# A two-layer hybrid block on one core: attention woven into its own input projection, state matrices made in pieces, four-pass products made three rounded ones, one more weight buffer

## The chip, the cores and the metric

The kernel runs on one core of one Trainium2 chip. The metric is the device time of one execution in microseconds (us), from several runs of the same program. TensorE (PE in the profile) multiplies, VectorE (DVE) and ScalarE (ACT) do the element-wise work, GpSimd (POOL) clears buffers and issues a few transfers, SyncE (SP) issues the weight transfers.

## The reference, cut to what matters

Two layers work on 528 tokens (16 meta tokens and 512 inputs) of width 1024, all in 32-bit floats. Each layer is a mixer of three parallel parts, and an MLP with a squared ReLU:

```python
for l in range(2):
    a = rms_norm(h, norm_pre_mix[l])
    u, q, k, v, cq, ckv, kr = split(a @ w_in[l])          # 1024 -> 1376 columns
    y_ssm = s5_mixer(u, valid, ...)                       # linear recurrence, 16 groups x 64 states
    y_swa = swa_attention(q, k, v, sinks)                 # 8 heads, window 128, ALiBi, sinks
    y_mla = mla_mixer(cq, ckv, kr, pos, ...)              # 4 heads, low-rank q and kv, rope, causal
    mixed = concat(rms_norm(y_ssm), rms_norm(y_swa), rms_norm(y_mla))
    h = h + rms_norm(mixed @ w_out[l])                    # 1024 -> 1024
    a = rms_norm(h, norm_pre_mlp[l])
    h = h + rms_norm(square(relu(a @ w_mlp_up[l])) @ w_mlp_down[l])   # 1024 -> 4096 -> 1024
```

## The kernel before, in words

Tokens lie along the free axis, in two halves: A (272 tokens) and B (256). A weight matrix is cut into blocks of 128 output columns; a block is 8 tiles of 128x128, fetched by two transfers of 256 KB (`raw`). Per layer and half there are 11 blocks of input projection (`w_in`), 8 of output projection (`w_out`), and four MLP chunks of 8 blocks up and 8 down.

`gemm` (L137 to L163) computes one block in one of two ways. Where its input is plain 32-bit (`exact`), TensorE multiplies 8 pairs of tiles straight from `raw` (L153), in four passes each; the trace counts two records for one such product. Otherwise weight and input are each held as a rounded high part and a rounded rest, and TensorE does three products for each pair, 24 for a block (L161). `load_half` then has to split each half block of weights: ACT writes the rounded high part (L124, `w<-raw`), DVE the rest (L133). An input made for rounded products costs one or two more element-wise operations as well (`split`, L165 to L171).

The exact way is chosen by the tables at the top: FULL_IN (input projection of A and B in layer 0; of A the first NF = 9 blocks), FULL_OUT (output projection of A in both layers), FULL_C0 (first MLP chunk of A in both layers). That makes 33 exact blocks of 272 columns (9 + 8 + 8 + 3 + 5) and 35 of 256 (11 + 8 + 8 + 5 + 3).

`s5_prep` makes the state matrices and tables of the recurrence from the parameters alone, mostly with small DVE operations and a few PE transposes and products. It is called as one piece after the input projection of A (in `main`'s loop). `s5_half` (recurrence of one half) and `attn_half` (both attentions of one half) are generators: `weave` advances them beside a main stream of blocks, each by a rate (RS, RA) per block of the main stream. `weave(s1())` runs the input projection of B in layer 0 (WB = 11 blocks), or the second to fourth MLP chunk of B of layer 0 (`late`, 48 blocks, of which 6 run earlier) in layer 1, with the sides of half A; `weave(s2())` runs A's output projection, its residual and norms (`chain_mid`), the input projection of B in layer 1, and A's first MLP chunk, with the sides of half B. Sides begin only when the gate's stage is reached.

The order in each engine's queue is made by the framework's scheduler from the order in which the code issues, with a higher priority for the weight splits (HW) and for the norm chains (HP). Each engine then works through its queue in that order.

Of the kernel before, what the change touches and what calls it, by code (L numbers as in the profile page):

```python
# [20 lines left out]
P = 128  # L21
# [46 lines left out]
def hybrid(ctx, tc, xT, wblk, small, wglu, wuq, wukv, bD, cD, ident_d, bias_d, tbias_d, mask_d, rope_d, tau_d, outT):  # L68
# [7 lines left out]
    wsp = ctx.enter_context(tc.tile_pool(name="wsp", bufs=3))  # L76
# [102 lines left out]
    def tmp_p():  # L179
        return mk(wk, [P, 2, 272], F32, "wP", bufs=3)  # L180
# [59 lines left out]

    def s5_prep(L):
        l = L["l"]
# [4 lines left out]
        exp_acc(step, a, (s1, s2))  # L247
        V.tensor_tensor(a, sm(l, "are"), step, op=ALU.mult)
        exp_acc(r, a, (s1, s2))
        V.tensor_tensor(a, sm(l, "aim"), step, op=ALU.mult)  # L250
# [6 lines left out]
        V.tensor_tensor(plo, a, phi, op=ALU.subtract)  # L257
        tab = mk(mem, [P, 2, 8, TAB], F32, "tab")
# [7 lines left out]
        for i0 in range(0, 8, 4):  # L266
# [8 lines left out]
            V.scalar_tensor_tensor(x, km, MAGIC, x, op0=ALU.subtract, op1=ALU.subtract)  # L275
        act(tab[:, 0], tab[:, 1], AF.Sin, scale=TWO_PI / 2)
# [26 lines left out]
        V.tensor_tensor(ci, ci, den, op=ALU.mult)  # L303

# [18 lines left out]
        rs = mk(mem, [P, 8 * 68], F32, "rs")  # L323
        braw = flat(tmp_p(), 512).rearrange("p (c i j) -> p c i j", c=2, i=8)
# [3 lines left out]
        nci = chain_tmp()[0][:, :256].rearrange("p (i j) -> p i j", i=8)  # L328
        V.tensor_scalar(nci, vt[:, CL - 1, 1], -1.0, None, op0=ALU.mult)
        t3 = mk(psm, [P, 512], F32, "y")  # L330
        for i0 in range(0, 8, 4):
# [11 lines left out]
            for j in range(4):  # L343
                i = i0 + j
                for c, rhs in enumerate((vt[:, CL - 1, 0, i, :], nci[:, i, :])):
                    PE.matmul(t3[:, 32 * i:32 * i + 32], lhsT=ws[c][:, j].rearrange("p a b -> p (a b)"), rhs=rhs,
                              start=c == 0, stop=c == 1)
        t3v = t3[:, :256].rearrange("p (i j) -> p i j", i=8)
        act(tt[:, :, 3, :], t3v)
        for so in range(3):  # L350
            for q in range(so + 1):
                f = 32 * (q + 3 - so)
                act(tt[32 * q:32 * q + 32, :, so, :], t3v[f:f + 32])
        for m in range(CL):
# [3 lines left out]
        L["s5"] = dict(r4=r4, rs=rs, tab=tab, wt=wt, vt=vt, tt=tt)  # L358
# [26 lines left out]
    def new_layer(l):  # L385
        L = dict(l=l)
# [10 lines left out]
        return L  # L397

    def w_in(L, hf, ar, M):
# [5 lines left out]
        M["hf"] = hf  # L405
# [11 lines left out]
        for b in range(NB_IN):  # L417
            if l + hf == 0 and b == NF:
# [35 lines left out]
            yield  # L454
# [22 lines left out]
    def s5_half(L, M):  # L477
        l, hf = L["l"], M["hf"]
# [3 lines left out]
        tab, rs, r4 = s5["tab"], s5["rs"], s5["r4"]  # L482
        rv = rs[:, :8 * K].rearrange("p (i k) -> p i k", i=8)
        V.tensor_copy(rv, r4.unsqueeze(2).to_broadcast([P, 8, K]))
        V.memset(rv[:, :, 0:1], 0.0)
# [17 lines left out]
        for o in range(2):  # L503
# [13 lines left out]
            if hf == 1:  # L517
                it = mk(tiny, [P, 2, 4], F32, "init", bufs=1)
                for c in range(2):
                    V.tensor_tensor(it[:, c], sv[:, c, iq], r4[:, iq], op=ALU.mult)  # L520
                    w0 = iv(w_)[:, c, :, 0]
                    V.tensor_tensor(w0, w0, it[:, c], op=ALU.subtract if c else ALU.add)
            yield 2.7
            for c in range(2):
                V.tensor_tensor_scan(v_[:, c, :n], rs[:, 4 * o * K:4 * o * K + n], w_[:, c, :n], 0.0, op0=ALU.mult, op1=ALU.add)
# [75 lines left out]
    def attn_half(L, M):  # L601
        l, hf = L["l"], M["hf"]
# [21 lines left out]
        yield 0.5  # L624
        wq = []
# [23 lines left out]
        yield 1.0  # L649
        vt = mk(psm, [P, 512], F32, "s")  # L650
# [9 lines left out]
        units = [("swa", j, o, g) for j, o, _ in full for g in range(4)] + ([("swah", 0, 0, 0)] if head else [])  # L660
# [132 lines left out]
    def w_out(l, hf, mixed, o, b0, b1):  # L793
        n = span(l, hf)[1]
        for b in range(b0, b1):
            ps, = gemm(l, NB_IN + b, [(mixed, n)])
            act(o[:, b, :n], ps[:, :n])
            yield
# [28 lines left out]
    def up(l, c, st, b0=0, b1=8):  # L827
# [3 lines left out]
        for b in range(b0, b1):  # L831
# [10 lines left out]
            yield  # L842

    def down(l, c, st, b0=0, b1=8):
        for b in range(b0, b1):
# [7 lines left out]
            yield  # L853
# [22 lines left out]
    def weave(main, sides):  # L876
        due = [0.0 for _ in sides]
        for ready in main:
            for i, (g, rate, gate) in enumerate(sides):
                if ready < gate:  # L880
                    continue
                due[i] += rate
                while due[i] > 0:
                    c = next(g, None)
                    due[i] = -1e9 if c is None else due[i] - c
# [206 lines left out]
```

## Time and profile before

| what | value |
|---|---|
| median of 3 runs | 1330.17 us (1327.77 to 1330.74) |
| profiled execution | 1329.14 us, span 1327.3 us |
| PE busy | 1255.9 us, 95% of the span |
| DVE busy | 811.8 us, 61% |
| ACT busy | 793.1 us, 60% |
| mean granted PE clock | 0.978 of full speed |

The profiled execution is 1.0 us under the median. The span runs from the first to the last instruction; 1.8 us lie around it. PE, DVE and ACT work side by side, so their busy times do not add up; a stretch of the program takes at least as long as its busiest engine.

### The profile page before, as it was taken

Reading aid. Unit: us, or ns where it says so; the run is one execution under the profiler, and the core shown is the slowest. Engines: PE = TensorE matmul, PEld = TensorE weight load, DVE = VectorE, ACT = ScalarE, POOL = GpSimd, SP = SyncE. Lnnn points to the kernel's source line nnn. Section 1 sums busy time; section 2 is a strip of 40 time slices with the busy share of each in tenths; the row PEclk is TensorE's granted clock in tenths of the full one; section 3 lists DMA queues with packets and bytes.
Section 4 is the critical chain, followed back from the end, with each engine's and each line's share of the span. In section 5 each row is a group of like instructions: output and inputs, shape, how many; then the busy total and the mean of one; then the engine's idle time right before and its main releaser. Section 6 shows DMA issues by size and latency. Waiting matters only on the chain.

```text
span 1327.3 us, 26248 instructions
## 1 busy us (share of the span) xinstructions
PE 1255.9 (95%) x9784; PEld 1135.4 (86%) x9784; DVE 811.8 (61%) x2134; ACT 793.1 (60%) x1876; POOL 32.2 (2%) x66
## 2 busy tenths in 40 slices
PE   6899999799999999899999997999999999999995
PEld 5767775679999999898899987867789999999985
DVE  7766456475756566869777667454475333334776
ACT  5347647675866656756687656387666542534663
POOL 4001000010000000000000000000000000000000
PEclk9989999899999999899999998999999999999998
DMA  7322231235666666463344644312446433334663
GB/s 227 119 61 69 88 88 57 64 111 170 181 182 176 176 172 177 130 178 107 108 142 131 174 144 142 105 59 77 132 131 184 118 89 95 96 91 122 186 183 95
DMA packets 93231, 170.47 MB, mean 128 GB/s; under 512 B 10960, under 2 KB 14032, under 8 KB 93104
## 3 DMA queue, kind: packets, MB, share of 16 engines
q1 hardware_dynamic: 90288, 161.62, 42.0%
q0 software_dynamic: 2816, 7.18, 1.7%
q8 instruction: 77, 1.26, 0.4%
q14 instruction: 50, 0.41, 0.1%
HBM read 166.66 MB, written 2.10 MB: 127 GB/s over the span
## 4 chain that ended last, share of the span: by engine, by line
PE 83%; DVE 10%; ACT 5%; issue 1%; DMA 0%; DVEq 0%; ACTq 0%; POOLq 0%
PE d L161 47%; PE d L153 14%; PE bu L161 7%; PE o L754 3%; PE s L674 2%; PE pt L730 2%; ACT ch L124 2%; DVE big L781 2%; DVE h L782 2%; PE s L706 1%; ACT slot L124 1%; PE s L640 1%; DVE ch L198 1%; PE bu L508 1%; PE o L203 1%
## 5 line engine op out<-in xcount | busy, mean ns | idle before, releaser
L161 PE MATMUL d<-slot,w 128*128 128x256 f32 (+1 forms) x5568 | 702.4, 286 | 20.7 <-DVE slot L422 6.7
L161 PEld LDWEIGHTS d<-slot,w 128*128 128x128 f32 x5568 | 682.9, 191 | 31.6 <-ACT ch L124 6.9
L124 ACT ACTIVATE w<-raw 128x512 fp32r<-128x512 f32 x464 | 291.9, 629 | 271.6 <-PE d L161 192.0
L133 DVE TENSOR_TENSOR w<-raw,w 128x512 fp32r<-128x512 f32 x464 | 320.7, 692 | 211.1 <-ACT w L124 204.8
L153 PE MATMUL d<-slot,raw 128*128 128x256 f32 (+1 forms) x1088 | 273.3, 396 | 11.3 <-ACT ch L124 10.2
L153 PEld LDWEIGHTS d<-slot,raw 128*128 128x128 f32 x1088 | 205.3, 194 | 52.3 <-ACT ch L124 10.2
L161 PE MATMUL bu<-slot,w 128*128 128x256 f32 x768 | 93.5, 282 | 0.0
L161 PEld LDWEIGHTS bu<-slot,w 128*128 128x128 f32 x768 | 92.0, 190 | 0.0
L168 DVE TENSOR_TENSOR slot<-rl,slot 128x256 fp32r<-128x256 f32 (+1 forms) x112 | 47.3, 428 | 66.5 <-ACT slot L124 65.7
L198 DVE TENSOR_TENSOR ch<-ch 128x256 f32<-128x256 f32 (+1 forms) x112 | 48.1, 430 | 28.3 <-ACT ch L124 26.4
L124 ACT ACTIVATE rl<-d 128x256 f32<-128x256 f32 (+1 forms) x112 | 42.1, 376 | 34.4 <-PE d L153 17.6
L124 ACT ACTIVATE slot<-rl 128x256 fp32r<-128x256 f32 (+3 forms) x128 | 52.9, 421 | 2.8
L124 ACT ACTIVATE slot<-h,small 128x256 fp32r<-128x256 f32 (+3 forms) x88 | 39.8, 506 | 15.9 <-DVE h L782 12.2
L124 ACT ACTIVATE ph<-pt 128x512 f32<-128x512 f32 (+2 forms) x66 | 36.7, 556 | 20.4 <-PE pt L730 12.2
L124 ACT ACTIVATE rl<-rl 128x256 f32<-128x256 f32 (+1 forms) x112 | 46.1, 420 | 2.1
L852 DVE TENSOR_TENSOR big<-d,big 128x256 f32<-128x256 f32 (+1 forms) x80 | 34.3, 429 | 15.9 <-PE d L161 12.1
L674 PE MATMUL s<-kv,slot 128*128 128x512 f32 (+1 forms) x64 | 32.0, 582 | 0.8 <-ACT vs L124 0.7
L124 ACT ACTIVATE big<-d 128x256 f32<-128x256 f32 (+1 forms) x64 | 24.0, 375 | 13.7 <-PE d L153 7.3
L124 ACT ACTIVATE ch<-big 128x256 f32<-128x256 f32 (+1 forms) x64 | 26.4, 415 | 9.6 <-DVE big L852 7.4
L124 ACT ACTIVATE ch<-h 128x256 f32<-128x256 f32 (+1 forms) x64 | 24.9, 415 | 8.2 <-DVE ch L198 4.5
L782 DVE SCALAR_TENSOR_TENSOR h<-big,small,h 128x256 f32<-128x256 f32 (+1 forms) x64 | 28.5, 486 | 0.0
L706 PE MATMUL s<-kv,slot 96*128 96x264 f32 (+3 forms) x80 | 26.5, 413 | 0.3 <-DVE mx L585 0.3
(603 smaller groups left out, 1135.7 us busy)
## 6 DMA issues: line engine op xcount, KB each, us to landing
raw<-in_wblk SPq DMA_DIRECT2D x600, 256.0 KB, 2.7
ph<-in_wuq POOLq DMA_DIRECT2D x8, 256.0 KB, 3.0
h<-in_xT SPq DMA_DIRECT2D x4, 272.0 KB, 3.9
h<-in_xT SPq DMA_DIRECT2D x1, 1024.0 KB, 11.6
ph<-in_wukv POOLq DMA_DIRECT2D x4, 256.0 KB, 3.0
u<-in_wglu POOLq DMA_DIRECT2D x4, 256.0 KB, 3.0
out<-h SPq DMA_DIRECT2D x1, 1024.0 KB, 5.6
out<-h SPq DMA_DIRECT2D x4, 256.0 KB, 2.2
```

The source lines that it names most:

```text
L124: S.activation(out, in_, func, **kw)
L133: V.tensor_tensor(w[:, 1].rearrange("p k m -> p (k m)"), raw, f32(hi), op=ALU.subtract)
L153: PE.matmul(ps[:, :n], lhsT=raw[:, k * P:(k + 1) * P], rhs=a[:, 4 * q + k, :n], start=q + k == 0, stop=q + k == 4)
L161: PE.matmul(ps[:, :n], lhsT=w[:, wi, k, :], rhs=a[:, ai, 4 * q + k, :n], start=i == 0, stop=i == 23)
L168: V.tensor_tensor(lo, src, f32(hi), op=ALU.subtract)
L198: V.tensor_tensor(acc, acc, sq, op=ALU.add)
L674: PE.matmul(sp[:, :2 * nk].rearrange("p (e k) -> p e k", e=2), lhsT=M["q"][:, c0:c0 + P], rhs=L["k2"][:, :, ks:ks + nk], start=True, stop= ...
L706: PE.matmul(sp, lhsT=M["qh"][0:96, 2 * g + e, o:o + P], rhs=L["kh"][:, 2 * g + e, c0:c1], start=True, stop=True)
L730: PE.transpose(pt[:, 256 * x + P * e:256 * x + P * e + P], vs[e][:, c0:c0 + P], ident)
L754: PE.matmul(ops[64 * e:64 * e + 64, :P], lhsT=v, rhs=pp[:, P * e:P * e + P], start=i == 0, stop=i == len(ph) - 1, tile_position=(0, 64 * e))
L782: V.scalar_tensor_tensor(h[hf][:, k, o:o + n], src[:, k, :n], sm(l, gn, k), h[hf][:, k, o:o + n], op0=ALU.mult, op1=ALU.add)
L852: V.tensor_tensor(ac[:, b, :n], ps[:, :n], ac[:, b, :n], op=ALU.add)
```

## The change

- FULL_IN keeps only A of layer 0 (its first 9 blocks); FULL_OUT and FULL_C0 are empty. So 24 blocks of 272 columns and 35 of 256 go from eight four-pass products to 24 rounded ones, and their weights are split.
- The split weights have four buffers in place of three (`wsp`); one scratch buffer of the recurrence is given up for it (`tmp_p`), its factor row `rs` is made per half of the groups, and `s5_prep` uses parts of `vt` as scratch.
- `s5_prep` is a generator. In layer 0 it is a side of the first weave, ahead of `s5_half`; in layer 1 it is a side of the MLP stream that ends layer 0 (rate RP).
- The input projection of A is now the head of the first weave's main stream, and `attn_half` begins inside it: `wait` holds a side until the blocks that it needs are issued. ORD sets the order of blocks: for A the latent and key blocks first, the recurrence's (0, 1) last; for B the value block (10) ahead of the queries. Attention units go group by group.
- In layer 0 one block of B's input projection is left for after A's output projection (WB = 10). Side steps are paid by estimated time of the main stream (`cost`), with new rates.

```diff
-FULL_IN = ((0, 0), (0, 1))
-FULL_OUT = ((0, 0), (1, 0))
-FULL_C0 = ((0, 0), (1, 0))
-RS = ((2.4, 1.5), (0.75, 2.2))
-RA = ((2.76, 2.5), (0.92, 3.5))
+FULL_IN = ((0, 0),)
+FULL_OUT = ()
+FULL_C0 = ()
+RS = ((1.6, 0.5), (0.8, 0.8))
+RP = 0.25
+RA = ((0.8, 1.6), (0.35, 1.2))
+ORD = ((2, 3, 4, 5, 10, 6, 7, 8, 9, 0, 1), (0, 1, 2, 3, 4, 5, 10, 6, 7, 8, 9))
-WB = (11, 0)
+WB = (10, 0)
...
-    wsp = ctx.enter_context(tc.tile_pool(name="wsp", bufs=3))
+    wsp = ctx.enter_context(tc.tile_pool(name="wsp", bufs=4))
...
     def s5_prep(L):
+        yield 0.0
...
         exp_acc(step, a, (s1, s2))
+        yield 3.0
...
-        braw = flat(tmp_p(), 512).rearrange("p (c i j) -> p c i j", c=2, i=8)
+        braw = vt[:, 1]
...
-        for b in range(NB_IN):
-            if l + hf == 0 and b == NF:
+        for bi, b in enumerate(ORD[hf]):
+            if l + hf == 0 and bi == NF:
                 a, _ = gains(l, hf, 0, n, "g_in", False)
             ps, = gemm(l, b, [(a, n)])
...
-            yield
+            M["done"].add(b)
+            yield cost(l, hf, FULL_IN, n) if bi < NF or l + hf else cost(l, hf, (), n)
+
+    def cost(l, hf, full, n):
+        return 8 * (0.42 * 4 * n + 3 if (l, hf) in full else 1.26 * n + 28) / 1e3
+
+    def wait(M, *need):
+        while not set(need) <= M.get("done", set()):
+            yield None
...
     def attn_half(L, M):
+        yield from wait(M, 2)
...
-        units = [("swa", j, o, g) for j, o, _ in full for g in range(4)] + ([("swah", 0, 0, 0)] if head else [])
+        units = [("swa", j, o, g) for g in range(4) for j, o, _ in full] + ([("swah", 0, 0, 0)] if head else [])
...
             if u is not None:
+                yield from wait(M, 5, *([6 + u[3]] if u[0] == "swa" else [6, 7, 8, 9]))
                 pend.append([u, first(u), None])
...
-        for ready in main:
+        for ready, us in main:
             for i, (g, rate, gate) in enumerate(sides):
                 if ready < gate:
                     continue
-                due[i] += rate
+                due[i] += rate * us
...
-        run(w_in(L, 0, aA, M[0]))
-        if l == 0:
-            nc.sync.dma_start(out=h[1], in_=xT[1][:, :, :HN[1]])
-        s5_prep(L)
+        winA = w_in(L, 0, aA, M[0])
+        wA = next(winA)
...
         def s1():
+            yield 0, wA
+            yield from staged(0, winA)
+            if l == 0:
+                nc.sync.dma_start(out=h[1], in_=xT[1][:, :, :HN[1]])
...
-        weave(s1(), ((s5_half(L, M[0]), RS[l][0], 0), (attn_half(L, M[0]), RA[l][0], 0)))
+        weave(s1(), ((seq(L["prep"], s5_half(L, M[0])), RS[l][0], 0), (attn_half(L, M[0]), RA[l][0], 0)))
...
-            s5_ok = 3 if WB[l] == NB_IN else 2 if WB[l] >= 2 else 1
+            s5_ok = 3
...
-        run(mlp(l, CA[l] + 1, CZ[l], [A, B]), mlp(l, CZ[l], NCH, [A]))
+        rest = seq(mlp(l, CA[l] + 1, CZ[l], [A, B]), mlp(l, CZ[l], NCH, [A]))
+        weave(staged(0, rest), ((layers[l + 1]["prep"], RP, 0),) if l < DEPTH - 1 else ())
```

On PE in the input projection of A in layer 0 the queue before holds projection products only (`d<-slot,raw`; `slot` is the normed input, the last number is the columns).

```order
L153 MATMUL d_182<-slot_110,raw_183 128x272 x4
L153 MATMUL d_182<-slot_110,raw_189 128x272 x4
L153 MATMUL d_196<-slot_110,raw_197 128x272 x4
L153 MATMUL d_196<-slot_110,raw_203 128x272 x4
L153 MATMUL d_217<-slot_110,raw_218 128x272 x4
L153 MATMUL d_217<-slot_110,raw_224 128x272 x4
L153 MATMUL d_231<-slot_110,raw_232 128x272 x4
L153 MATMUL d_231<-slot_110,raw_238 128x272 x4
```

In the changed kernel the same place, from the fourth block on, holds attention's first products among them (`s` and `pt`: keys and values from the latent; `o<-am,ones`: a norm's column sum).

```order
L155 MATMUL d_448<-slot_110,raw_449 128x272 x4
L155 MATMUL d_448<-slot_110,raw_455 128x272
L636 MATMUL s_242<-slot_151,ph_229 128x272
L641 MATMUL pt_250<-ph_229,slot_151 16x256
L155 MATMUL d_448<-slot_110,raw_455 128x272 x2
L636 MATMUL s_246<-slot_151,ph_229 128x272
L641 MATMUL pt_253<-ph_229,slot_151 128x256
L205 MATMUL o_414<-am_411,ones 128x272
L207 MATMUL o_414<-am_411,ones 128x272
L641 MATMUL pt_256<-ph_229,slot_151 128x256
L155 MATMUL d_448<-slot_110,raw_455 128x272
```

Attention's work of half A has moved ahead by the whole projection, and stands between exact products.

On DVE in the input projection of B in layer 0 the queue before has no weight splits (`wP`, `wQ`: the recurrence's scratch; `am`: a norm of attention).

```order
L422 TENSOR_TENSOR slot_709<-d_712,rc_699 128x64x4
L213 SCALAR_TENSOR_TENSOR am_784<-o_786,am_784 128x272
L214 TENSOR_SCALAR am_784<-am_784 128x272
L215 TENSOR_TENSOR am_784<-am_784 128x272
L613 SCALAR_TENSOR_TENSOR slot_151<-slot_151,small_92,am_784 128x272
L513 TENSOR_TENSOR wP_775<-bu_766,tab_444 128x544
L514 TENSOR_TENSOR wQ_776<-bu_766,tab_444 128x544
```

In the changed kernel the same work on `wP` and `wQ` follows weight splits (`w<-raw,w`) and a softmax step (`s__203`).

```order
L135 TENSOR_TENSOR w_1229<-raw_1227,w_1229 128x512
L200 TENSOR_TENSOR ch_1180<-ch_1180 128x256
L603 ISA s__203_1122,mx_1124<-s_1123,mask 128x144
L603 ISA mx_1124 128x1
L135 TENSOR_TENSOR w_1295<-raw_1293,w_1295 128x512
L135 TENSOR_TENSOR w_1312<-raw_1310,w_1312 128x512
L237 TENSOR_TENSOR ps_796_4717<-ps_796_4717,pstep_4718 128x8
L527 TENSOR_TENSOR wP_1046<-bu_1037,tab_288 128x544
L528 TENSOR_TENSOR wQ_1047<-bu_1037,tab_288 128x544
```

The splits of the next blocks now share DVE's queue with attention and the recurrence.

On PE after A's output projection in layer 0 the queue before goes from attention's last products straight to A's first MLP block (`d_2376`); the two column sums of norms (L203) stand in between.

```order
L706 MATMUL s_2263<-kv_144,slot_709 128x400
L754 MATMUL o_2279<-ph_2171,vs_145 64x128
L754 MATMUL o_2406<-ph_2273,vs_145 64x128 x4
L706 MATMUL s_2290<-kv_144,slot_709 128x400
L203 MATMUL o_2421<-am_2413,ones 128x256
L730 MATMUL pt_2392<-ident,s__441_2255 128x128
L203 MATMUL d_2368<-ch_2351,ones 128x272
L153 MATMUL d_2376<-slot_2342,raw_2377 128x272 x4
```

In the changed kernel the last block of B's input projection (`d_2686`, 24 products) stands there, ahead of A's first MLP blocks (`d_2802`, `d_2912`).

```order
L566 MATMUL y_2554<-wP_2461,vt_349 32x64
L205 MATMUL o_2620<-ch_2604,ones 128x272
L566 MATMUL y_2554<-wP_2461,vt_349 32x64 x7
L163 MATMUL d_2686<-slot_1163,w_2689 128x256 x12
L163 MATMUL d_2686<-slot_1163,w_2706 128x256 x12
L751 MATMUL pt_2740<-ident,s__415_2311 128x128 x4
L695 MATMUL s_2723<-kv_144,slot_1206 128x512
L163 MATMUL d_2802<-slot_2644,w_2805 128x272
L163 MATMUL d_2912<-slot_2644,w_2915 128x272
```

One block and part of half B's attention have moved into the place of the norm chain.

## Rows read from the trace of the kernel before

**Rows 1.** The page: span, PE's busy time, and the chain by engine.

```profile
span 1327.3 us, 26248 instructions
...
PE 1255.9 (95%) x9784; PEld 1135.4 (86%) x9784; DVE 811.8 (61%) x2134; ACT 793.1 (60%) x1876; POOL 32.2 (2%) x66
...
PE 83%; DVE 10%; ACT 5%; issue 1%; DMA 0%; DVEq 0%; ACTq 0%; POOLq 0%
```

**Rows 2.** Stretches: from:to, us, busy by engine (PE, PEld, DVE, ACT, POOL), clock, DMA.

```profile
10.21:47.88 37.67, 36.57 (x146) 29.54 (x147) 33.76 (x169) 18.88 (x37) 4.51 (x10) 1.00 0.61 185
47.88:70.07 22.19, 15.22 (x103) 14.27 (x101) 15.98 (x69) 9.95 (x25) 1.04 (x2) 0.79 0.24 80
70.07:154.76 84.69, 84.26 (x683) 64.01 (x681) 53.22 (x203) 50.50 (x152) 4.98 (x10) 0.98 0.27 76
154.76:241.59 86.83, 76.33 (x625) 53.02 (x617) 47.53 (x166) 56.60 (x167) 3.89 (x7) 0.94 0.22 65
241.59:301.82 60.23, 60.23 (x314) 46.69 (x313) 33.38 (x120) 38.59 (x85) 3.42 (x7) 0.97 0.35 103
301.82:344.34 42.52, 42.14 (x279) 38.20 (x277) 29.48 (x64) 28.28 (x65) 0.00 (x0) 1.00 0.58 167
366.95:534.92 167.97, 167.75 (x1347) 166.89 (x1346) 101.29 (x167) 101.36 (x202) 0.00 (x0) 1.00 0.62 176
597.15:768.79 171.64, 168.61 (x1559) 156.08 (x1559) 128.02 (x356) 120.52 (x308) 2.18 (x4) 1.00 0.46 134
768.79:798.43 29.64, 28.59 (x134) 24.75 (x133) 19.12 (x48) 15.72 (x40) 1.04 (x2) 1.00 0.48 137
798.43:839.42 40.99, 34.08 (x270) 33.37 (x269) 30.35 (x64) 24.99 (x50) 0.00 (x0) 0.92 0.52 152
839.42:942.25 102.83, 101.46 (x786) 74.57 (x784) 48.67 (x172) 67.26 (x184) 1.11 (x2) 1.00 0.25 75
942.25:1032.54 90.29, 84.57 (x633) 80.62 (x632) 57.52 (x115) 59.61 (x134) 0.00 (x0) 0.98 0.54 156
231.00:241.59 10.59, 2.44 (x6) 1.52 (x6) 8.88 (x25) 8.79 (x23) 0.00 (x0) 0.51 0.00 0
```

**Rows 3.** PE in order of time: start, us, line, operation, records; undisturbed block streams.

```profile
22.31 25.93 PE L153 MATMUL d<-slot,raw 128*128 128x272 f32 x112 [1.10 <-DVE slot L422]
...
770.97 15.70 PE L153 MATMUL d<-slot,raw 128*128 128x256 f32 x72
...
438.14 48.49 PE L161 MATMUL d<-slot,w 128*128 128x272 f32 x384
...
301.82 22.78 PE L161 MATMUL d<-slot,w 128*128 128x256 f32 x192
```

**Rows 4.** PE in order of time between the two input projections of layer 0.

```profile
69.05 1.22 PE L203 MATMUL d<-ch,ones 128*128 128x256 f32 x2 [4.34 <-DVE ch L198]
```

**Rows 5.** Groups by line and form: count, busy us, mean ns, idle before.

```profile
L161 PEld LDWEIGHTS d<-slot,w 128*128 128x128 f32 x5568 | 682.9, 191 | 31.6 <-ACT ch L124 6.9 <-ACT rl L124 6.5 <-DVE w L133 5.4
...
L133 DVE TENSOR_TENSOR w<-raw,w 128x512 fp32r<-128x512 f32 x464 | 320.7, 692 | 211.1 <-ACT w L124 204.8
L124 ACT ACTIVATE w<-raw 128x512 fp32r<-128x512 f32 x464 | 291.9, 629 | 271.6 <-PE d L161 192.0 <-PE bu L161 44.5 <-DMA raw<-in_wblk 13.7
...
L168 DVE TENSOR_TENSOR slot<-rl,slot 128x256 fp32r<-128x256 f32 x88 | 36.7, 424 | 53.9 <-ACT slot L124 53.2
...
L124 ACT ACTIVATE slot<-rl 128x256 fp32r<-128x256 f32 x88 | 35.7, 417 | 1.7
...
L171 DVE SCALAR_TENSOR_TENSOR slot<-h,small,slot 128x256 fp32r<-128x256 f32 x32 | 14.0, 489 | 0.0
...
L124 ACT ACTIVATE slot<-big,small 128x256 fp32r<-128x256 f32 x16 | 7.4, 501 | 3.8 <-DVE big L473 3.8
```

**Rows 6.** Who waited for whom: total us, times, longest.

```profile
DVE w L133 <- ACT w L124: 204.8, 309, 2.6
ACT w L124 <- PE d L161: 192.0, 226, 4.0
```

More of the change, by code (lines that the diff above doesn't have):

```diff
@@ L179, in tmp_p @@
     def tmp_p():
-        return mk(wk, [P, 2, 272], F32, "wP", bufs=3)
+        return mk(wk, [P, 2, 272], F32, "wP", bufs=2)
     def tmp_q():
@@ L404, in scaled @@
             V.tensor_tensor(out, ps, r[:, :out.shape[1]], op=ALU.mult)
-        M["hf"] = hf
+        M["hf"], M["done"] = hf, set()
         M["y"] = mk(mem, [P, KD, 272], F32, f"big{hf}")
@@ L477, in s5_half @@
     def s5_half(L, M):
+        yield from wait(M, 0, 1)
         l, hf = L["l"], M["hf"]
@@ L624, in attn_half @@
         yield 0.5
+        yield from wait(M, 3, 4)
         wq = []
@@ L649, in attn_half @@
         yield 1.0
+        yield from wait(M, 10)
         vt = mk(psm, [P, 512], F32, "s")
@@ L841, in up @@
                 split(x["f"][:, 0, b, :n], x["f"][:, 1, b, :n], f[:, :n])
-            yield
+            yield sum(cost(0, 0, ((0, 0),) if x["full"] else (), x["n"]) for x in st)
     def down(l, c, st, b0=0, b1=8):
@@ L852, in down @@
                     V.tensor_tensor(ac[:, b, :n], ps[:, :n], ac[:, b, :n], op=ALU.add)
-            yield
+            yield sum(cost(0, 0, ((0, 0),) if x["full"] else (), x["n"]) for x in st)
     def chain_end(l, hf, x, tag):
@@ L881, in weave @@
                     continue
-                due[i] += rate
+                due[i] += rate * us
                 while due[i] > 0:
-                    c = next(g, None)
-                    due[i] = -1e9 if c is None else due[i] - c
-        live = [g for g, _, _ in sides]
-        while live:
-            live = [g for g in live if next(g, None) is not None]
-    def staged(stage, gen):
-        for _ in gen:
-            yield stage
-    layers = [None] * DEPTH
+                    c = next(g, -1.0)
+                    if c is None:
+                        due[i] = 0.0
+                    else:
+                        due[i] = due[i] - c if c >= 0 else -1e9
+        for g, _, _ in sides:
+            for c in g:
+                assert c is not None
+    def staged(stage, gen):
+        for us in gen:
+            yield stage, us
+    layers = [dict(l=l) for l in range(DEPTH)]
+    for L in layers:
+        L["prep"] = s5_prep(L)
     def seq(*gens):
@@ L941, in s1 @@
                 for _ in range(WB[l]):
-                    next(winB[0])
-                    yield 0
-        weave(s1(), ((s5_half(L, M[0]), RS[l][0], 0), (attn_half(L, M[0]), RA[l][0], 0)))
+                    yield 0, next(winB[0])
+        weave(s1(), ((seq(L["prep"], s5_half(L, M[0])), RS[l][0], 0), (attn_half(L, M[0]), RA[l][0], 0)))
         def s2():
```

32 lines of the change are left out of this document (19 added, 13 removed).

## The prediction, as put on record

> **What bounds the kernel now.** I read the page first, for which engine is full and which ends the chain; then busy time by stretch, because an average hides stages with different limits; then PE in order of time for the price of a block and for the holes; then the groups by line for the price of the added work. The page says PE: it is busy 1255.9 of 1327.3 us, and 83% of the chain is PE's [rows 1]. DVE and ACT are at 61% and 60%, so on average there is room for more element-wise work. By stretch that room is uneven [rows 2]. Where a half's attention runs (70 to 302 us, 597 to 769, 839 to 942) PE is nearly full, DVE and ACT at 45 to 75%. PE waits in four places: 7.0 us of 47.88 to 70.07, where the state matrices are made; 8.2 us of 231.00 to 241.59, the norm chain of half A in layer 0; 6.9 us of 798.43 to 839.42, the same chain in layer 1; and 5.7 us of 942.25 to 1032.54. The granted clock is 0.79 in the first and 0.51, near the lower level of 1.2 GHz, in the second, so work around a hole runs slowly as well.
>
> **What the change takes from PE.** Blocks are priced from undisturbed streams [rows 3]. An exact block of 272 columns is 25.93/7 = 3.70 us (16 records a block, 112 in the row), a rounded one 48.49/16 = 3.03: 0.67 less. At 256 columns it is 15.70/4.5 = 3.49 against 22.78/8 = 2.85: 0.64 less. 24 blocks of 272 and 35 of 256 change: 16.2 + 22.4 = 38.6 us. Every one stands in a stretch where PE is at 88% or more, so I count all of it as on the path as long as PE stays the limit.
>
> The Trainium skill (FP8 and Floating Point Precision, TensorE Precision Notes) gives four passes for true FP32, so three rounded products would save a quarter. By that rule a block would fall by 1.01 and 0.95 us, 57.5 us together, and the time would be 1285. The rows show a ratio of 1.22, not 1.33, and decide.
>
> The hole at the state matrices: PE waits there on DVE, 4.34 us in the longest wait [rows 4]. Spread over the projection of A, that work stands beside exact products, which need no splits. What can come back is 7.0 us idle and 3.2 us of slow clock (15.22 busy at 0.79), from 0 to 10.2; I take 8, near the top, because 37.67 us of projection lie beside it with PE 97% busy and the products there wait for nothing that DVE does late. In layer 1 the same work moves from the stretch at 597 into 366.95 to 534.92, where DVE and ACT stand at 60%: its PE part is paid in either place, so 0.
>
> The hole of the norm chain (8.2 us) gets one block of B's projection, 2.85 us; attention that was late could fill more, or the block could itself be late. From 0 to 8.2; I take 2.9. In layer 1 half B's attention may start beside B's projection, not after it: this can return up to the 1.4 + 5.7 us idle in 839 to 1033; I take 2, since the second of these is a norm chain that stays. Reordered blocks and units, and the smaller scratch, change no count of PE work: 0.
>
> Sum on PE: 38.6 + 8 + 2.9 + 2 = 51.5 us. The profiled execution took 1329.1, so PE alone would give 1277.6.
>
> **What it adds to DVE and ACT, and what is late next.** 59 blocks bring 118 splits, each 0.692 us on DVE and 0.629 on ACT [rows 5]: 81.7 and 74.2 us. The MLP's middle values of 16 blocks need a rounded part and a rest (0.42 and 0.42 each), the head norm of 16 row blocks one more on each (0.50 ACT, about 0.42 DVE), the input of B eight rests more (0.49). Against that, A's MLP input is no longer made twice, 16 ACT operations of about 0.5 fewer. Together about +96 us on DVE and +81 on ACT. This costs nothing only while PE's work hides it.
>
> Layer 0 up to 344.34 is where it piles up. DVE has 213.4 us there in the six rows from 10.21 [rows 2]; 35 blocks add 70 x 0.692 + 8 x 0.424 + 8 x 0.42 + 16 x 0.489 = 63.0, making 276.4. ACT goes from 202.8 to 254.1 in the same way. PE would want this stretch, 334.1 us long, to take 334.1 - 23.2 - 8 - 2.9 = 300.0. That would be 92% of DVE and 85% of ACT, in order, with chains between them. The highest share of DVE in a long row is 90% (10.21 to 47.88, mostly work with no partner), the highest with attention beside rounded blocks 75% (597 to 769), and there PE set the pace, so 75% is no limit. I take 86%, nearer to the fuller row: 276.4/0.86 = 321.4, so 21.4 us are given back. The ends are 0 (92% reached) and 36 more than before (75%).
>
> Queued behind a late split on DVE are the evacuations and norms that free PSUM and slots; PE waits for the split itself. The fourth buffer lets splits run one half block further ahead. At present ACT's splits wait 192.0 us in total for PE to free a buffer [rows 6], so buffers do limit the lead; but PE waited for DVE's splits only 5.4 us in all [rows 5], and a lead is worth nothing where DVE is short on average. I value it at 0, between 0 and those 5.4 us.
>
> In layer 1, 768.79 to 1032.54, 24 blocks go from 263.8 to 246.4 us by PE, with 195.7 of DVE (79%) and 201.1 of ACT (82%). Only 839.42 to 942.25 is tight: ACT 67.3 + 16.4 + 3.3 = 86.9 of 94.5 us, 92%; at 88% it takes 98.8 and gives back 4.3 (from 0 to 12).
>
> Total: 1277.6 + 21.4 + 4.3 = 1303.3; the profiled execution lies 1.0 under the median, so I predict 1304 us, 2% faster.
>
> A rule of the skill speaks against the change (Perfetto Trace Analysis, Identifying the Most-Contended Engine): PE is better judged by how full weight loading is than by matmul time. In the rounded stream PEld is full (166.89 of 167.97), among exact blocks with attention 64.01 of 84.69 [rows 2]; a rounded block loads 24 tiles where an exact one shows 16. By this rule attention's products would no longer find loading free. The rows bound it: 42 rounded blocks (119.6 us) leave 49.0 us of PE for a half's attention at 597 to 769, 11 exact ones (38.4) leave 45.9 at 70 to 155, so 3 us a half and 9 for three halves: 1313.
>
> **Rivals.** First, splits stay hidden and PE alone sets the time: 1279. For it: DVE and ACT idle 40% today, and 75% of DVE left PE 98% busy. Against: 92% over 300 us has no row. Second, slower: DVE's queue in layer 0 becomes the limit and its chains leave it idle a quarter of the time. At 78% the stretch takes 354.4 us, 20.3 more than before, layer 1 gains 13, the time is 1337; at the 75% of the row 1372, layer 1 then losing 6. The sign turns at 276.4/347.2 = 80%. For it: attention's softmax and norms are DVE-ACT-PE-DVE loops, and each engine keeps its order. Against: those loops now run beside three times as many blocks. Third, attention inside A's projection makes PE wait in its queue for each norm, and the 8 us of the first hole return as small waits: 1312. Against: among exact blocks at 70 to 155 such steps left PE idle 0.4 us. Fourth, weight loading as above, 1313. Fifth, the splits eat just what the products save (DVE at 80 to 81%), the change does nothing: 1330.
>
> **How the numbers follow.** My forecast with the third and fourth rival, which lie in its own range of 1285 to 1322: 0.58. PE alone, below 1285: 0.19. Small gain, 1322 to 1327: 0.05. No change: 0.04. Slower: 0.14, half of it above 1338. The range 1268 to 1338 leaves out that half and a few in a hundred below, where the waits at both norm chains would vanish too. A measurement of this kernel tells about 0.2% from no change; faster by more is 0.58 + 0.19 + 0.05 = 0.82, within 0.04, slower 0.14.
>
> **What would show it.** In the changed profile exact products are 9 blocks (144 records), PE's busy time is about 1215 us, DVE's about 905 and ACT's 875. A's projection in layer 0 takes some 55 to 65 us with attention's products in it and no wait over 3 us. Right on the splits: DVE is 83 to 89% busy between the first product and the first MLP chunk of B (then near 330 us), PE waits there in many short pieces for `w` from DVE, and the granted clock stays above 0.9. PE alone is right if that share is over 90%, the slower rival if it is under 80% with PE idle for over 50 us. The forecast is wrong if the stretch from 10 us to B's first MLP chunk does not get shorter, or if layer 1's 24 blocks do not save at least 8 us.

## The result, and the profile after

The changed kernel takes 1293.32 us (median of 4 runs, 1292.39 to 1296.66) against 1330.24 on the same chip: ratio 0.9731 [0.9709, 0.9752], 2.7% faster. Its profiled execution is 1293.41 us, its span 36.0 us shorter than before.

The page of the changed kernel, with the lines that answer to [rows 1]:

```profile
span 1291.3 us, 27666 instructions
...
PE 1215.4 (94%) x10256; PEld 1131.5 (88%) x10256; DVE 886.2 (69%) x2300; ACT 850.0 (66%) x2010; POOL 32.2 (2%) x66
...
PE 46%; DVE 5%; ACT 3%; issue 1%; DMA 1%; DVEq 0%; ACTq 0%
```

PE's busy time fell by 40.5 us and the span by 36.0, so PE now idles 75.9 us, 4.5 more than before. The chain of waits is followed only part of the way (its shares add up to little over half), so stretches say more. The changed kernel's, columns as in [rows 2]: layer 0 from the first product to B's first MLP chunk; the place of A's norm chain in it; layer 1 from A's output projection to the end of A's part of the first chunks; and a hole in that.

```profile
10.77:312.98 302.21, 289.88 (x2435) 245.09 (x2436) 255.31 (x875) 235.74 (x607) 18.13 (x35) 0.99 0.38 112
142.10:201.12 59.02, 57.39 (x600) 47.79 (x598) 44.76 (x139) 45.08 (x123) 3.04 (x5) 1.00 0.35 109
735.54:999.38 263.84, 239.60 (x2008) 218.16 (x2007) 184.99 (x456) 187.16 (x452) 2.15 (x4) 0.94 0.42 121
766.02:800.00 33.98, 21.25 (x184) 19.06 (x183) 25.02 (x64) 16.27 (x40) 0.00 (x0) 0.70 0.19 56
```

The first stretch took 334.1 us in the six rows from 10.21 [rows 2]: 31.9 came out of it, nearly the whole gain. PE idles 12.3 us there (19.4 before), the granted clock is 0.99, and both holes are gone: the second row's stretch holds A's output projection and its norm chain with 1.6 us idle. The third stretch took 263.8 us before, as one row:

```profile
768.79:1032.54 263.75, 248.70 (x1817) 213.31 (x1816) 155.66 (x399) 167.59 (x406) 2.14 (x4) 0.98 0.42 122
```

It takes 263.8 now: nothing came out of it, although PE is busy 9.1 us less. The fourth row above holds the longest single wait in it. The changed kernel on PE, in order of time (start, us, line, operation, records, wait before it):

```profile
771.54 1.41 PE L163 MATMUL d<-slot,w 128*128 128x256 f32 x9
785.07 1.08 PE L508 MATMUL y<-slot,ident 128*32 128x64 f32 x32 [12.12 <-DVE slot L430]
786.08 1.01 PE L163 MATMUL d<-slot,w 128*128 128x256 f32 x3
```

And on DVE at the same time:

```profile
775.06 0.76 DVE L803 TENSOR_TENSOR big<-big,ch 128x256 f32<-128x256 f32 x2
775.74 0.87 DVE L804 SCALAR_TENSOR_TENSOR h<-big,small,h 128x256 f32<-128x256 f32 x2
...
780.92 3.25 DVE L173 SCALAR_TENSOR_TENSOR slot<-h,small,slot 128x256 fp32r<-128x256 f32 x8
...
784.42 0.59 DVE L430 TENSOR_TENSOR slot<-d,rc 128x256 f32<-128x256 f32 x1
```

Read them together. The recurrence's first small product (L508) stands in PE's queue ahead of the next block and needs an evacuation (L430) of B's projection. That evacuation stands on DVE behind a norm chain: eight pairs of L803 and L804, then eight L173, the rounded rests, which stand in this chain because A's MLP blocks behind it are now rounded (the kernel before makes them later, from 986 us on). In 769 to 786 us PE waits 12.1 us in one piece, and the granted clock of the stretch around it is 0.70. In the kernel before, without rests in the chain, PE waits for the same evacuation (who waits for whom, total us, times, longest):

```profile
PE d L161 <- DVE slot L422: 6.7, 1, 6.7
```

So the wait is 5.4 us longer now, but it was there before.

### The profile page after: what moved, and what is told of

Its sections match the earlier page's. It is cut to its first block, busy times and chain, and to the rows that moved or that the text cites. A ratio compares the mean times of both kernels' runs of the same rounds, so it can differ in the third digit from the quotient of the medians.

```text
span 1291.3 us, 27666 instructions
## 1 busy us (share of the span) xinstructions
PE 1215.4 (94%) x10256; PEld 1131.5 (88%) x10256; DVE 886.2 (69%) x2300; ACT 850.0 (66%) x2010; POOL 32.2 (2%) x66
## 4 chain that ended last, share of the span: by engine, by line
PE 46%; DVE 5%; ACT 3%; issue 1%; DMA 1%; DVEq 0%; ACTq 0%
PE d L163 32%; PE bu L163 7%; PE o L775 1%; DVE h L804 1%; DVE big L803 1%; PE pt L751 1%; PE s L695 1%; ACT ch L126 1%; DVE w L135 1%; ACT w L126 1%; PE s L727 1%; DMA raw<-in_wblk 1%; PE bu L522 1%; DVE slot L173 1%; PE o L205 0%
## 5 line engine op out<-in xcount | busy, mean ns | idle before, releaser
L163 PE MATMUL d<-slot,w 128*128 128x256 f32 (+1 forms) x6984 | 913.1, 288 | 27.9 <-ACT rl L126 7.6
L163 PEld LDWEIGHTS d<-slot,w 128*128 128x128 f32 x6984 | 865.5, 190 | 53.1 <-issue 10.1
L135 DVE TENSOR_TENSOR w<-raw,w 128x512 fp32r<-128x512 f32 x582 | 400.0, 690 | 210.0 <-ACT w L126 201.5
L126 ACT ACTIVATE w<-raw 128x512 fp32r<-128x512 f32 x582 | 363.9, 627 | 261.6 <-PE d L163 180.9
L170 DVE TENSOR_TENSOR slot<-rl,slot 128x256 fp32r<-128x256 f32 (+1 forms) x128 | 54.0, 427 | 58.0 <-ACT slot L126 56.3
L126 ACT ACTIVATE slot<-rl 128x256 fp32r<-128x256 f32 (+1 forms) x128 | 52.6, 419 | 2.6
L155 PE MATMUL d<-slot,raw 128*128 128x272 f32 x144 | 38.6, 413 | 10.8 <-DMA raw<-in_wblk 10.8
L874 DVE TENSOR_TENSOR big<-d,big 128x256 f32<-128x256 f32 (+1 forms) x80 | 34.3, 429 | 15.7 <-PE d L163 12.1
L155 PEld LDWEIGHTS d<-slot,raw 128*128 128x128 f32 x144 | 28.1, 200 | 17.6 <-ACT ch L126 10.7
L126 ACT ACTIVATE slot<-h,small 128x256 fp32r<-128x256 f32 (+2 forms) x72 | 33.0, 505 | 15.0 <-DVE h L804 10.8
L126 ACT ACTIVATE ch<-h 128x256 f32<-128x256 f32 (+1 forms) x64 | 25.3, 413 | 10.8 <-DVE ch L200 9.6
L804 DVE SCALAR_TENSOR_TENSOR h<-big,small,h 128x256 f32<-128x256 f32 (+1 forms) x64 | 28.4, 480 | 0.0
L173 DVE SCALAR_TENSOR_TENSOR slot<-h,small,slot 128x256 fp32r<-128x256 f32 (+1 forms) x64 | 27.9, 481 | 0.0
```

The costliest lines, as they stand in the source:

```text
L126: S.activation(out, in_, func, **kw)
L135: V.tensor_tensor(w[:, 1].rearrange("p k m -> p (k m)"), raw, f32(hi), op=ALU.subtract)
L155: PE.matmul(ps[:, :n], lhsT=raw[:, k * P:(k + 1) * P], rhs=a[:, 4 * q + k, :n], start=q + k == 0, stop=q + k == 4)
L163: PE.matmul(ps[:, :n], lhsT=w[:, wi, k, :], rhs=a[:, ai, 4 * q + k, :n], start=i == 0, stop=i == 23)
L170: V.tensor_tensor(lo, src, f32(hi), op=ALU.subtract)
L173: V.scalar_tensor_tensor(lo, src, gain, f32(hi), op0=ALU.mult, op1=ALU.subtract)
```

## The experiments

Each kernel differs from the changed one (in one case from the one before) by the edit shown. They ran on several chips, each beside the kernel before, so what a part is worth is a difference of ratios times 1330 us. By the intervals of the two ratios such a difference is good to 4 or 5 us.

**The order without the products.** The three tables are those of the kernel before.

```diff
-FULL_IN = ((0, 0),)
-FULL_OUT = ()
-FULL_C0 = ()
+FULL_IN = ((0, 0), (0, 1))
+FULL_OUT = ((0, 0), (1, 0))
+FULL_C0 = ((0, 0), (1, 0))
```

> The changed kernel with the three tables of before: the 59 blocks are exact again, everything else as changed (woven order, state matrices in pieces, fourth weight buffer). Theory (order and products both count, the order by filling PE's holes in layer 0, the products in layer 0 alone): 23 us of layer 0's products come back, those of layer 1 bring nothing, so about 1316. Rival 1 (all of the gain is the products, 38.6 us; the order only rearranges): 1328 to 1332. Rival 2 (the order alone gives the gain, products are paid back by splits everywhere): 1290 to 1297.

1302.47 us, 0.9810 [0.9776, 0.9844], outside all three. Its page:

```profile
span 1300.4 us, 26265 instructions
...
PE 1245.3 (96%) x9784; PEld 1126.9 (87%) x9784; DVE 805.1 (62%) x2142; ACT 789.9 (61%) x1877; POOL 32.2 (2%) x66
```

Its layer 0 up to B's first MLP chunk:

```profile
10.60:319.10 308.50, 304.69 (x2134) 238.57 (x2134) 208.85 (x784) 200.57 (x530) 17.88 (x34) 1.00 0.38 110
```

The order and the fourth buffer alone take 25 us off. PE idles 3.8 us in 308.5. Over the whole span its busy time is 10.6 us under that of before for the same products, at a mean clock of 0.986 against 0.978.

**The products without the order.** The kernel before, with the changed kernel's three tables.

> The kernel before with the three tables of the change alone: 59 blocks rounded, old order, three weight buffers. Theory: PE still idles in layer 0's two holes, longer in the norm chains since 8 rests more stand in each, and about 10 to 15 of the 38.6 us are left: 1315 to 1320. Rival 1 (all is the products): 1293 to 1298. Rival 2 (products are paid back by splits): 1328 or more.

1344.65 us, 1.0114 [1.0099, 1.0129]: 15 us slower than before, as rival 2 had it. Two of its stretches, the state matrices and A's output projection with the norm chain:

```profile
47.90:73.00 25.10, 17.41 (x110) 16.41 (x110) 21.41 (x105) 13.02 (x31) 1.04 (x2) 0.75 0.35 104
151.30:247.20 95.90, 81.75 (x648) 59.60 (x648) 66.31 (x214) 70.88 (x199) 3.83 (x7) 0.86 0.21 61
```

Its waits (who waits for whom, total us, times, longest):

```profile
PE d L161 <- DVE w L133: 12.1, 7, 4.8
...
PE d L161 <- DVE slot L422: 10.4, 1, 10.4
PE s L706 <- DVE mx L585: 8.7, 5, 6.0
```

The second stretch is 9 us longer than its like before, and PE idles 14.2 us in it against 10.5 [rows 2], at a clock of 0.86 against 0.94. Its longest wait there is the 6.0 us for a softmax step (`mx`), which stands on DVE behind half A's norm chain; the eight rests at that chain's end (L171, 3.4 us) came into it with the rounded products. The 10.4 us are the same in layer 1, for an evacuation, and the 4.8 us there are a wait for a weight split itself. On the span PE is busy 15.6 us less than before and idle 29.4 more. So the products cost 15 us in the old order with three buffers, and give some 10 (0.9810 to 0.9731) in the new one with four.

**Three weight buffers.**

```diff
-    wsp = ctx.enter_context(tc.tile_pool(name="wsp", bufs=4))
+    wsp = ctx.enter_context(tc.tile_pool(name="wsp", bufs=3))
```

> The changed kernel with three buffers for split weights. Theory: a rounded block of 256 columns costs 2.84 us in steady streams with three buffers and 2.80 with four, so with some 70 such blocks and the pairs in the last MLP chunks about 3 to 5 us more: 1296 to 1299; the stretch from the first block for both halves (999) to the end grows from 291.9 to about 294.8. Rival (the lead is worth nothing): 1293, that stretch 291.9.

1304.60 us, 0.9816 [0.9799, 0.9833]: the buffer is worth 11 us, more than both theories had. The stretch from A's first MLP chunk to B's, in this kernel:

```profile
202.80:320.60 117.80, 110.36 (x795) 97.96 (x796) 94.33 (x265) 93.70 (x223) 3.08 (x7) 0.93 0.38 107
```

In the changed kernel:

```profile
201.12:312.98 111.86, 104.78 (x792) 93.85 (x793) 93.19 (x264) 92.14 (x222) 3.10 (x7) 0.98 0.38 110
```

Idle is 7.4 and 7.1 us; the 6 us lie in PE's busy time, at a clock of 0.93 against 0.98. Layer 0 up to B's first chunk is 7.6 us longer in all. The stretch from the first block for both halves to the end takes 295.4 us against 291.9, as the theory had it; what the theory left out is layer 0.

**Layer 1 exact.** FULL_OUT and FULL_C0 are ((1, 0),), all else as changed.

> The changed kernel with A's output projection and first MLP chunk of layer 1 exact (24 blocks), layer 0 rounded. Theory (layer 1's rounded products bring nothing, their saving is lost in the norm chain of half A, which got eight rests on DVE, and behind it): 1290 to 1297, PE's long wait after A's output projection falls from 12.1 to about 9 us. Rival (they bring the 15.4 us that the block prices say): 1306 to 1310.

1296.89 us, 0.9741 [0.9714, 0.9769]: not told apart from the changed kernel. Its stretch of layer 1:

```profile
735.40:999.00 263.60, 250.44 (x1816) 215.45 (x1815) 154.17 (x402) 166.92 (x407) 2.13 (x4) 0.97 0.41 123
```

PE is busy 10.8 us more and idle 11.1 less (13.2 against 24.2), over the same 263.6 us: layer 1's rounded products bring nothing. The long wait is shorter here, by 4.8 us, and so by less than half of the idle time that went:

```profile
PE y L508 <- DVE slot L430: 7.3, 1, 7.3
```

**The evacuations first.** In layer 1 B's evacuations get a higher priority.

```diff
+HE = 200
...
+            with tc.high_priority(offset=HE if hf and l else 0):
+                if b < 2:
+                    V.tensor_tensor(M["u"][:, b, :n]...
```

> In layer 1 the evacuations of B's projection blocks get a higher priority, so that on DVE they stand ahead of most of half A's norm chain. Theory A (TensorE's queue is held for 12.1 us at 773 to 785 us because an evacuation stands behind that chain on DVE, and layer 1's gain went there): the hole shrinks to under 4 us and the time falls by 6 to 12 us, to 1281 to 1288 us. Rival B (the vector engine has that work to do in any case, and TensorE then waits for the norm chain's end instead): the hole moves to A's first MLP chunk, time 1291 to 1296 us.

1291.85 us, 0.9721 [0.9703, 0.9738]. The wait:

```profile
PE y L510 <- DVE slot L432: 4.2, 1, 4.2
```

The place of the hole:

```profile
769.50:778.41 8.91, 4.28 (x61) 3.73 (x59) 7.22 (x17) 4.64 (x10) 0.00 (x0) 1.00 0.55 149
```

The wait fell from 12.1 to 4.2 us, near the 4 of theory A; the time, 1291.85, is in rival B's range and did not follow by a size that the intervals can tell. Nor did the hole move to one other place, as rival B had it: the next wait in the stretch is 2.6 us long. The stretch of layer 1:

```profile
737.00:994.34 257.34, 238.42 (x2009) 216.33 (x2007) 183.76 (x456) 186.67 (x452) 2.14 (x4) 0.96 0.43 125
```

It takes 257.3 us in this profile, but four kernels below with layer 1 as changed, wait of 12.1 us included, take 258.0, 258.1, 261.8 and 263.0. So how much of the 263.8 is the hole and how much the clock (0.94 there, 0.97, 0.96, 0.95 and 0.94 in the four) stays open.

**Attention after the projection, for both halves.**

```diff
-        yield from wait(M, 2)
+        yield from wait(M, *range(NB_IN))
```

> Attention of a half begins only when all 11 blocks of its own projection are issued, in both layers; all else as in the changed kernel. Theory A (the order's 27 us come from attention begun early, which fills the hole of the state matrices and lets the rest of layer 0 start sooner): some 8 to 20 us slower, 1301 to 1313 us. Rival B (the order's gain is the fourth weight buffer, the pieces and the block left for the norm chain; where attention begins does not matter): 1290 to 1297 us.

1362.36 us, 1.0263 [1.0243, 1.0283], far over theory A. The stretch that grew, in its layer 0:

```profile
244.70:343.26 98.56, 78.39 (x464) 56.30 (x463) 53.56 (x221) 64.41 (x165) 2.55 (x6) 0.81 0.16 46
```

The edit holds half B's attention too, and one of B's blocks is left for after A's output projection: all of it then came behind that block, 20 us of PE idle at a clock of 0.81. This run does not price half A's early start, so the next one was made.

**Half A alone.**

```diff
-        yield from wait(M, 2)
+        yield from wait(M, *(range(NB_IN) if M.get("hf") == 0 and L["l"] == 0 else (2,)))
```

> Only half A of layer 0 holds its attention until its whole input projection is issued; half B and layer 1 are as in the changed kernel. Theory A (from the run before, where A's output projection began only 1.8 us later: beginning half A's attention early is worth little, because the pieces of the state matrices fill that place): 1293 to 1298 us. Rival B (it is worth 8 us or more, and the run before hid that): 1301 to 1308 us.

1324.13 us, 0.9958 [0.9943, 0.9972]: 30 us of the 37 are gone, so rival B, and more. The figure of 1.8 us in theory A was misread: in the run before, A's output projection began at 147.8 us with a few products, and 164 of its 192 ran only from 170.7 us on. Two stretches, from the end of A's exact blocks to B's first block, and on to where A's output projection gets under way:

```profile
56.81:78.37 21.56, 16.95 (x164) 14.93 (x163) 18.03 (x50) 6.61 (x14) 1.04 (x2) 0.75 0.35 108
78.37:173.43 95.06, 86.45 (x910) 69.45 (x906) 75.80 (x287) 70.13 (x203) 6.09 (x12) 0.98 0.27 79
```

The same two run from 73.00 to 146.01 in the changed kernel: A's projection ended earlier here, but the output projection, which needs all of half A's attention, came 27 us later.

**State matrices in one piece**, after A's projection in layer 0 (`whole` runs all of `s5_prep` in one step).

```diff
-        weave(s1(), ((seq(L["prep"], s5_half(L, M[0])), RS[l][0], 0), ...
+        weave(s1(), ((seq(*((wait(M[0], *range(NB_IN)), whole(L["prep"])) if l == 0 else (L["prep"],)), s5_half(L, M[0])), RS[l][0], 0), ...
```

> In layer 0 the state matrices are made in one piece once all of A's projection is issued, as in the kernel before; attention still begins early. Theory A (the hole was 22.2 us long with 7.0 us of TensorE idle, and the pieces took it away): TensorE idles 5 to 15 us more before B's projection, time 1298 to 1308 us. Rival B (attention's products and the split weights now fill that place in any case): 1290 to 1297 us.

1310.26 us, 0.9864 [0.9849, 0.9879]: 18 us over the changed kernel, theory A and 2 us more. From B's first block to A's second output block, in this kernel:

```profile
85.00:160.00 75.00, 68.34 (x762) 60.18 (x762) 62.65 (x200) 46.82 (x119) 1.66 (x3) 0.89 0.28 83
```

And in the changed kernel:

```profile
88.28:146.01 57.73, 54.73 (x608) 47.70 (x606) 52.40 (x173) 41.29 (x104) 1.66 (x3) 1.00 0.34 102
```

Here 154 more records of PE stand in the stretch (the matrices' and the recurrence's, which had to wait for them), 3.7 us more of it are idle, and the clock is 0.89.

**No block left.** WB is (11, 0).

> All 11 blocks of B's projection in layer 0 run before A's output projection; none is left for A's norm chain. Theory A (the left block covers the hole that was 8.2 us of TensorE idle at 231 to 242 us): that hole comes back with 4 to 9 us, time 1297 to 1302 us. Rival B (half B's attention covers it): 1290 to 1296 us.

1307.71 us, 0.9847 [0.9824, 0.9870], 15 us over the changed kernel and above both theories. From A's last output block (206 us) to its first MLP block:

```profile
206.10:226.00 19.90, 15.18 (x159) 8.87 (x159) 14.40 (x42) 14.12 (x34) 2.55 (x4) 0.79 0.27 81
226.00:236.00 10.00, 6.95 (x29) 4.13 (x30) 8.41 (x24) 7.81 (x18) 0.00 (x0) 0.50 0.00 0
236.00:245.52 9.52, 7.96 (x20) 4.24 (x19) 5.71 (x18) 5.17 (x13) 0.00 (x0) 0.50 0.00 0
```

39 us in which PE has the recurrence's last small products, up to 210 us, and then little but attention's last units, with a softmax between their products; the clock is 0.50 (1.2 GHz) for the last 20. In the changed kernel 8.8 us lie there. A left block also holds back attention: units wait for the query blocks, and the left block (9) is one of them, so those units run beside A's MLP blocks. The next run takes these two apart.

**Attention held, no block left.**

```diff
-WB = (10, 0)
+WB = (11, 0)
...
+                M[1]["done"].discard(9)
...
-            A.update(chain_mid(l, 0, o, "d" if WB[l] == NB_IN else "o"))
+            A.update(chain_mid(l, 0, o, "o"))
+            if WB[l]:
+                M[1]["done"].add(9)
```

> All 11 blocks of B's projection run ahead of A's output projection, as in the run that left none, but the last group of half B's attention units and its latent units are held until A's norm chain is issued, as the left block holds them in the changed kernel; the chain's column sums use the same buffer as in the changed kernel. Theory A (what leaving the block is worth is that it holds back attention, which then runs beside A's first MLP blocks and not before them): 1292 to 1299 us. Rival B (the 24 products of the block itself cover the chain): 1304 to 1309 us.

1301.76 us, 0.9785 [0.9767, 0.9803], between the two theories: holding attention back (with the column sums' other buffer) recovers 8 us of the 15, and the block itself is worth the other 7.

**More work on DVE.**

```diff
+            TW[0] -= 1
+            if q == 0 and TW[0] >= 0:
+                V.tensor_tensor(w[:, 1].rearrange("p k m -> p (k m)"), raw, f32(hi), op=ALU.subtract)
```

> In the first 45 blocks of layer 0 that take rounded weights, VectorE computes the rest of one of the two halves of a block twice (the same values again): 45 x 0.67 us = 30 us more on DVE before B's first MLP chunk, where it is now busy for 255.3 of 302.2 us. Nothing is changed on TensorE. Theory A (in layer 0 VectorE's queue now sets the pace, so that work put on it is paid for): 15 to 30 us slower, 1308 to 1323 us. Rival B (VectorE's 47 us of idle time take it up, and TensorE's own work is the limit): 1293 to 1299 us.

1308.27 us, 0.9847 [0.9823, 0.9871], at theory A's lower end. Its layer 0 up to B's first MLP chunk:

```profile
10.98:332.29 321.31, 299.79 (x2414) 251.84 (x2414) 280.08 (x914) 241.97 (x611) 17.98 (x35) 0.96 0.35 106
```

24.8 us more on DVE made the stretch 19.1 us longer, though DVE had 46.9 us idle and PE's products are the same but for 24 small ones, which come after the stretch here: PE's busy time grew by 9.9 at a clock of 0.96, its idle time by 9.2. By the medians the cost is 15 us; in this profile layer 1 took 258.1 us and not 263.8.

**Both edits on layer 1.** Evacuations first and layer 1 exact.

> Both edits on layer 1 together: B's evacuations first on DVE, and layer 1's 24 blocks exact as in the kernel before. Theory A (the 12 us hole goes, and the products bring nothing in layer 1, so the exact ones cost nothing and give VectorE and ScalarE back 48 half blocks of splitting): 1284 to 1291 us. Rival B (without the hole TensorE is the limit in layer 1, and the exact products cost there what the rounded ones save): 1293 to 1300 us.

1290.85 us (1289.49 to 1291.60), 0.9708 [0.9695, 0.9721]. It is the lowest median, but its interval overlaps the changed kernel's, so it is not shown to be faster. Nor is it slower than the evacuations first alone (0.9721), so rival B did not come: with the long wait cut to 3.1 us here and 4.2 there, rounded products still bring nothing in layer 1. Layer 1 in this kernel:

```profile
735.25:993.38 258.13, 248.52 (x1816) 213.76 (x1815) 154.09 (x402) 165.66 (x407) 2.13 (x4) 0.99 0.42 125
```

PE is 96% busy there at a clock of 0.99, and idle 9.6 us, where the evacuations first with rounded products leave it idle 18.9.

## Why the prediction was right, and where it was not

The direction held, and 1293 lies in the range and in the forecast's own range of 1285 to 1322. That it is only 11 us under 1304 is in part luck. The terms give 12.7 us out of layer 0 (23.2 + 8 + 2.9 - 21.4) and 13.1 out of layer 1 (15.4 + 2 - 4.3); the profiles show 31.9, 0, and 4.1 elsewhere. One miss partly cancels the other.

**Blocks, 38.6 us.** PE's busy time is 1215.4, as forecast ("about 1215"), and the exact products are the forecast 144 records. But 10.6 of the 40.5 us less come with the order, not the products, since the order's own run has them at a higher clock, so the match is luck in part. The products took 29.9 us off PE and about 10 off the time. By the four passes of the Trainium skill (FP8 and Floating Point Precision, TensorE Precision Notes) PE would have lost 57.5 us to them, an estimate of the prediction; the runs stand nearer to the rows' 38.6. (Its 1.01 and 0.95 us are a third of the rounded block; a quarter of the exact one, 3.70 and 3.49, is 0.93 and 0.87, and 52.7 us together.) The condition, "as long as PE stays the limit", is the step that failed.

**Layer 0, DVE's share.** The step was 276.4 us of DVE at 86%, 321.4 us in all. It came to 255.3 at 84.5%, 302.2 us. The load was mis-sized by 21.1. The share was right in part by luck: 255.3 us are 85% also of the 300.0 that the prediction gave PE alone. Splits in this stretch went from 22 to 91. Before:

```profile
L133 DVE TENSOR_TENSOR w<-raw,w 128x512 fp32r<-128x512 f32 x22 | 15.2, 693 | 10.9 <-ACT w L124 10.9
```

After:

```profile
L135 DVE TENSOR_TENSOR w<-raw,w 128x512 fp32r<-128x512 f32 x91 | 61.8, 686 | 11.2 <-ACT w L126 10.7
```

That is 46.6 us against the 48.4 priced. Added up one by one, DVE's operations in the stretch went from 260.5 to 314.5 us, 54.0 more where 63.0 were priced. But the records of neighbouring operations overlap, and the busy time counts the overlap once: it rose by 41.9. So 12 of the 21.1 us come from adding single durations to a busy time. Over the span DVE came to 886.2 and ACT to 850.0, not to about 905 and 875.

The sign that PE waits there "in many short pieces" for `w` from DVE did not come either. PE's longest waits in the stretch, behind its first product (total us, times, longest):

```profile
PE d L163 <- ACT slot L126: 2.5, 3, 1.4
PE d L163 <- DVE slot L173: 2.4, 1, 2.4
PE d L163 <- ACT am L126: 1.7, 1, 1.7
PE d L163 <- DVE w L135: 1.0, 2, 0.8
```

The splits themselves are 1.0 us of 12.3 idle. The run with more work on DVE tests the step itself: with 280.1 us of DVE, close to the 276.4 forecast, the stretch took 321.3. From the order alone to the changed kernel DVE's load there rose by 46.5 us (208.85 to 255.31) and the stretch fell by 6.3 (308.50 to 302.21) where PE's blocks save 23.2: 16.9 us given back, 0.36 for each us on DVE. Half of it is idle time of PE (3.8 to 12.3 us), the rest is busy time that did not fall; some 3 us are 24 small products of layer 1's state matrices, which stand inside the stretch in the changed kernel alone. The next 24.8 us cost 19.1, 0.77 each, or 0.6 by the medians. That the price climbs as DVE fills is what two points suggest, not shown: the repeated rests also stand right ahead of the products that read them.

**The second rival** (DVE's queue turns the change slower) is what the products do in the old order with three buffers: 1344.65, inside its 1337 to 1372, with DVE at 76.5% of that stretch (259.9 of 339.6 us). Its sum is not borne out, though: the stretch grew by 5.5 us, not by 20 or more, and layer 1 lost 6.8 (270.5 us), which the rival had at its upper end alone. It did not happen in the changed kernel, where the new order and the fourth buffer came with the products; the prediction valued both at 0 beyond the holes.

**The state matrices' hole, 8 us.** The hole went, and making the matrices in one piece costs 18. But early attention was no term of its own: half A's in layer 0 is worth 30 us when taken away alone, with the rates of the sides left as they were. That is the largest term that the prediction put at nothing. A's projection took 77.5 us with attention in it (10.77 to 88.28), not 55 to 65; PE was busy there for all but 0.6 us, with no wait over 0.3 inside it, so the third rival did not happen either.

**The norm chain, 2.9 us.** Leaving the block is worth 15, of which holding attention back gives 8. The prediction saw 8.2 us of idle; before, the clock in its 10.6 us was 0.51, and with no block left the place takes 39 us and not 8.8.

**The fourth buffer, 0 us.** Worth 11. "A lead is worth nothing where DVE is short on average" was wrong at 84.5% of DVE. ACT's splits waited 203.1 us for PE with three buffers and 180.9 with four, and PE waited for DVE's splits 12.3 us and 6.0. Of the 11.5 us on the span 8.1 lie in PE's busy time (1223.5 against 1215.4), at a lower clock. That the lead covers the pieces where DVE is late would fit, but no run shows it.

**Layer 1, 13 us.** By the prediction's own test (at least 8 us) this step failed: 0. Its 4.3 us of give-back looked at shares by stretch, and PE idles 9 us more although DVE is 70% busy there (185.0 of 263.8 us). The wait of 12.1 us by queue order, which no share shows, is a part of it: 5.4 us over before, 4.8 over layer 1 exact. It is not the whole: with that wait cut to 4.2 and 3.1 us, rounded and exact products still take the same time, PE idle 18.9 and 9.6 us. Where the rest goes, in short waits, was not taken apart.

**Slips in the working.** The +96 us of DVE do not agree with the stretches, which add 63.0 and 40.0; 74.4 were measured. At 75% of DVE layer 0 grows by 34.4 us, not 36. The projection of A does wait for DVE, 1.1 us in its own row [rows 3]. And part of layer 1's state matrices is made before B's first MLP chunk in both kernels (on DVE from 270 us on before, from 242 now), not from 597 us on or in the MLP stream. None of these is a term of the sum.

**Weight loading.** The rule of the Trainium skill (Perfetto Trace Analysis, Identifying the Most-Contended Engine) was priced at 1313 in the prediction, from rows. PEld is at 88% of the span, 2 points over before; the stretches of layer 0 have it at 81% with PE at 96%, so no run here shows loading to be the bound, and none was made to exclude it.

The parts are not additive. Taken away one at a time they cost 30 (early attention), 18 (pieces), 15 (block and held attention), 11 (buffer) and 10 us (products), 84 in all, against a gain of 36. So the parts need each other: with one missing the others lose some of their worth too. The clock is lower around the place of each but the products (0.75, 0.89, 0.50 and 0.93).

## What to carry to other kernels

Price a trade of products for element-wise work together with the order in which both stand: the same tables cost 15 us in one order and gave 10 in the other, with one more buffer. Where queues run in order, look for the one small instruction that stands ahead of large ones and ask what its input waits behind on the other engine; shares of busy time do not show it. Then measure what the wait is worth: here it went from 12.1 to 4.2 us, and the time moved by less than the intervals can tell. A busy time counts overlapping records once, so durations of single operations added to it come out too high (54.0 us added up, 41.9 of busy time). Removing one part of a change at a time gives its worth only beside the others.

## What the runs showed of the hardware

The granted clock is low around each loss: 0.70 around the 12.1 us hole, 0.50 where attention's last units stand alone, and 0.93 where three buffers in place of four added 6 us with 0.4 us more idle time. Layer 1 as changed took 263.8, 258.1 and 258.0 us in three kernels, with PE idle 24.2, 23.8 and 24.9 us and busy 239.6, 234.3 and 233.1: the difference lies in PE's busy time, at clocks of 0.94, 0.96 and 0.97. Records of DVE's operations overlap: in layer 0 they add up to 314.5 us in 255.3 of busy time.
